# The up projection of a two-layer trunk's MLP as seven block products (Strassen) in place of eight, on one Trainium2 core

## The chip, the cores and the metric

One core of one Trainium2 chip. The time is the device time of one execution of the whole kernel in microseconds (us); the figure is the median of three runs. The engines are named as in the profile: PE multiplies matrices, PEld loads its weights, DVE works on vectors, ACT on activations and copies, POOL on simple vector operations, and SP issues transfers. Each runs its own list of instructions in order, and waits on semaphores of the others.

## The reference, cut to what matters

Two layers; each adds a mixer and a squared-ReLU MLP to a residual `h` of 1024 features and 800 tokens (528 + 272, with 16 meta tokens at the head of each sequence; the second layer's MLP computes the 768 tokens that are put out).

```python
for l in range(DEPTH):
    hn = rms_norm(h, norm_mix[l])
    ...
    h = h + (ym @ w_out[l]).astype(h.dtype)
    hn = rms_norm(h, norm_mlp[l])
    h = h + (jnp.square(jax.nn.relu(hn @ w_up[l])) @ w_down[l]).astype(h.dtype)
return rms_norm(h[:, N_META:], norm_final)
```

`w_up[l]` is 1024 x 4096, `w_down[l]` is 4096 x 1024, all float32.

## The kernel before

Features lie on the 128 partitions and tokens along the free dimension; a tensor of 1024 features is eight tiles `h[0]` to `h[7]` of 128 x 800 (layer 0) or 128 x 768 (layer 1). Tokens are worked on in two halves of 400 or 384 columns. A large product is exact to float32 by three float32r passes: each operand is split into a high part and a low rest (`xh`, `xl` for activations; `wh`, `wl` for weights), and a product is `wh.xh + wh.xl + wl.xh`, the three matmuls of L434, L435 and L436.

Weights come by `raw` (a ring `wr` of three buffers of 512 KB, loaded by a transfer that SP issues, L446), and `wsplit` (L415 to L421) makes `wh` by a copy on ACT (L419) and `wl` by a difference on POOL (L420). Both have rings of two buffers, so a third `wh` waits until PE has done its last matmul with the first. `product` collects its sums in one of three PSUM banks `mm` (a further ring of three is called `hb`) and hands the bank to an eviction.

`mlp` (L1104 to L1181) splits the eight tiles of `h` into `self.x` and goes through w_up's 4096 columns in eight blocks of 512 (four column tiles). `ups(b)` makes four tiles of u: 4 tiles x 2 halves x 8 k x 3 passes = 192 matmuls, an eviction by ACT (relu, L1123) and DVE (times the sum again, L1124), and a split of u by ACT (L1128) and POOL (L1129). `downs(b, us)` takes the 512 rows of w_down in four loads, 8 m x 2 halves x 4 k x 3 = 192 matmuls, and DVE adds each sum to `h[m]` (L1150). `ups(b + 1)` stands ahead of `downs(b)` in the program. The norm's factor is applied late: DVE sums the squares behind `ups(0)` (L1160 to L1164), multiplies `h` by its mean square (L1172), takes the reciprocal (L1173), and multiplies the finished sum by it (L1154).

In layer 0 `s5_setup(1)`, some 400 small operations, most on DVE, is issued behind `downs(0)`; `norm_in` of layer 1 follows as the tiles of `h` are finished, and in layer 1 `final` (L325 to L369) norms and stores them. The order of each engine's list is set at build time by a scheduler with a model of the timeline; buffers of the pools `h`, `m`, `u` and `t` (`FO`) and of the rings come free when their last reader is done.

Of the kernel before, what the change touches and what calls it, by code (L numbers as in the profile page):

```python
# [73 lines left out]
AP = [0, 0]  # L74

class Trunk:
# [82 lines left out]
        # scores of a chunk pair, block-diagonal: the blocks beside the diagonal stay zero  # L159
# [4 lines left out]
        # what leaves the chip for a while  # L164
# [19 lines left out]
        # s5 skip gains: (g2 h) rows, (l gp) columns  # L184
# [6 lines left out]
        # s5 step sizes over the states  # L191
# [9 lines left out]
        # lower bounds: softmax over the depth, running sum less the first  # L201
# [13 lines left out]
        # forget gate = hA*t + hB, key/2 = -hK*t + hK, with t = tanh(x/2)  # L215
# [6 lines left out]
        # rg-lru: softplus(-lambda) with log1p by its atanh series  # L222
# [23 lines left out]
    def gate_weights(self, l):  # L246
        """Block-diagonal gates: (i, d, r|i)."""
# [27 lines left out]
    def load(self):  # L275
        """The residual and the operands of the first w_in, half by half of the tokens."""
# [48 lines left out]
    def final(self, m, t):  # L325
        """The last norm, feature tile by feature tile as they are done."""
        nc = self.nc
        if m == 0:
            self.g = self.t("u", (128, D))
            nc.sync.dma_start(self.g[:], self.ins["norm_final"].rearrange("(a f) -> a f", a=1).to_broadcast([128, D]))  # L330
            self.done, self.early, self.sq = [], [], None
# [16 lines left out]
        if m == 3:  # L348
            for i in range(6):
                o = self.t("t", (128, 512))  # L350
                nc.vector.tensor_tensor(out=o[:], in0=turn(i, 0)[:], in1=self.g[:, 0:512], op=MULT)
                self.early.append(o)
        if m == KD - 1:
# [4 lines left out]
            st = self.t("t", (128, 6))  # L358
# [3 lines left out]
            for i in range(6):  # L362
# [9 lines left out]
    def split(self, k, y, gain, rs=None, n=T):  # L372
        """Operand k = y*gain (*rs) as two float32r parts that add up to it exactly."""
# [12 lines left out]
    def sumsq(self, ys, n=T):  # L386
        """The sum of squares over the partitions of all tiles, on every partition: two PSUM halves."""
# [38 lines left out]
    def product(self, w, xs, halves, evac):  # L426
        """evac(half, psum) with psum = sum over k of w[k].T @ x[k]; w: pairs of [128, 128] parts."""
# [13 lines left out]
    def fetch(self, name, l, c):  # L441
        """128 columns of a weight matrix of 1024 rows, split."""
# [8 lines left out]
    def project(self, l, cols, evacs):  # L451
        """Columns of w_in, 128 from each of cols."""
# [7 lines left out]
    def scaled(self, out):  # L460
        """Evacuation into out, times the tokens' 1/rms."""
# [5 lines left out]
    def gelu(self, x):  # L467
        """x becomes 2 gelu(x), by the tanh formula."""
# [89 lines left out]
    def to_tokens(self, src, dst, dstm):  # L558
        """[feature, token] to [token of a chunk pair, pair, feature]; the meta chunks apart."""
# [37 lines left out]
    def hgrn(self, l, FP, K2, Q, V):  # L597
        """FP: forget gates of both directions, K2: keys, Q, V; returns the heads' outputs, normed."""
# [636 lines left out]
```

## Time and profile before

| | |
|---|---|
| median of three runs | 2200.97 us (2198.35 to 2202.42) |
| span of the profiled execution | 2201.6 us |
| PE busy | 2087.4 us, 95% |
| DVE / ACT / POOL busy | 1118.9 / 753.8 / 811.9 us |
| mean granted clock of PE | 0.964 of full speed |
| matmuls in the trace, all parts | 14082 |
| w_up's three passes in layer 0's windows | 341 to 355 ns recorded each, overlapping |

Busy times are shares of the whole span, over stages with different limits. A record of a matmul is longer than the distance between two of them, because they are pipelined; the pace is the number of matmuls in a window. [...] In a timeline a row stands for one instruction or for several alike ("x3"); "idle before" is how long the engine had nothing to do, and which engine's instruction ended that.

### The profile page before, as it was taken

What the parts mean: (1) busy time and instruction counts of PE and PEld (TensorE: products, weight loads), DVE (VectorE), ACT (ScalarE), POOL (GpSimd) and SP (SyncE); (2) the same over time, 40 slices, a digit from 0 to 9 for tenths busy, and PEclk for the clock granted to TensorE, in tenths of its full rate; (3) what the DMA queues carried; (4) which work ended last, traced back from release to release, by engine and by line L of the source; (5) the groups of instructions that cost most, each with busy time, mean ns of one, the idle gap of its engine ahead of it and who ended that gap; (6) DMA issues with size and microseconds to landing.
All of it is one profiled execution on the core that took longest, in us unless ns stands there. A gap on an engine that the chain in (4) does not pass through costs nothing.

```text
span 2201.6 us, 34495 instructions
## 1 busy us (share of the span) xinstructions
PE 2087.4 (95%) x14082; PEld 1957.7 (89%) x14082; DVE 1118.9 (51%) x2258; ACT 753.8 (34%) x1141; POOL 811.9 (37%) x622
## 2 busy tenths in 40 slices
PE   8899899889989899999999999998998999999998
PEld 6889897677979899999998879886888999999997
DVE  6884748487657871221155855746368221112224
ACT  6233535454322232212225553436432122222222
POOL 1672112263433443333444213322434343434343
PEclk9899899899999999999999999998999999999998
DMA  5322111342211431122122113221321112122221
GB/s 182 96 81 76 38 40 56 101 129 57 68 48 58 109 119 58 58 64 61 58 95 78 57 37 97 74 59 48 113 79 58 58 58 68 59 67 65 60 67 68
DMA packets 230886, 160.74 MB, mean 73 GB/s; under 512 B 33270, under 2 KB 217784, under 8 KB 230728
## 3 DMA queue, kind: packets, MB, share of 16 engines
q1 hardware_dynamic: 229832, 156.95, 23.8%
q8 instruction: 111, 1.82, 0.4%
q10 hardware_dynamic: 896, 1.58, 0.2%
q14 instruction: 47, 0.39, 0.1%
HBM read 131.32 MB, written 27.18 MB: 72 GB/s over the span
## 4 chain that ended last, share of the span: by engine, by line
PE 60%; DVE 10%; ACT 2%; issue 1%; POOL 1%; DMA 1%; SPq 0%; DVEq 0%; POOLq 0%; ACTq 0%
PE mm L435 18%; PE mm L434 18%; PE mm L436 18%; PE hb L664 2%; PE hb L582 1%; DVE m L1163 1%; DVE h L1172 1%; PE rb L510 1%; DVE xl L379 1%; DVE m L1164 1%; DVE h L1154 1%; DVE r L1173 0%; DVE m L1124 0%; PE rb L862 0%; POOL wl L420 0%
## 5 line engine op out<-in xcount | busy, mean ns | idle before, releaser
L420 POOL TENSOR_TENSOR wl<-wr,wh 128x1024 fp32r<-128x1024 f32 (+3 forms) x214 | 479.3, 2240 | 1005.5 <-ACT wh L419 982.7
L434 PE MATMUL mm<-xh,wh 128*128 128x400 f32 (+3 forms) x2016 | 710.2, 354 | 33.1 <-DVE m L1124 11.1
L435 PE MATMUL mm<-xl,wh 128*128 128x400 f32 (+3 forms) x2016 | 713.9, 355 | 6.0 <-POOL xl L383 2.9
L436 PE MATMUL mm<-xh,wl 128*128 128x400 f32 (+3 forms) x2016 | 701.1, 349 | 0.7 <-POOL wl L420 0.5
L419 ACT ACTIVATE wh<-wr 128x1024 fp32r<-128x1024 f32 (+3 forms) x214 | 205.7, 962 | 764.9 <-PE mm L435 658.5
L434 PEld LDWEIGHTS mm<-xh,wh 128*128 128x128 f32 x2016 | 388.6, 193 | 52.7 <-DVE m L1124 14.1
L435 PEld LDWEIGHTS mm<-xl,wh 128*128 128x128 f32 x2016 | 389.1, 193 | 18.5 <-DVE xl L379 4.1
L436 PEld LDWEIGHTS mm<-xh,wl 128*128 128x128 f32 x2016 | 388.8, 193 | 8.9 <-POOL wl L420 0.9
L434 PE MATMUL mm<-u,wh 128*128 128x400 f32 (+1 forms) x1024 | 349.1, 341 | 6.2 <-DVE m L1124 6.2
L435 PE MATMUL mm<-u,wh 128*128 128x400 f32 (+1 forms) x1024 | 349.6, 341 | 0.0
L436 PE MATMUL mm<-u,wl 128*128 128x400 f32 (+1 forms) x1024 | 348.3, 340 | 0.0
L1150 DVE TENSOR_TENSOR h<-mm,h 128x400 f32<-128x400 f32 (+1 forms) x256 | 144.5, 565 | 331.2 <-PE mm L436 331.2
L1124 DVE TENSOR_TENSOR m<-m,mm 128x400 f32<-128x400 f32 (+1 forms) x128 | 71.1, 559 | 369.2 <-ACT m L1123 369.2
L434 PEld LDWEIGHTS mm<-u,wh 128*128 128x128 f32 x1024 | 193.3, 189 | 7.8 <-DVE m L1124 7.1
L435 PEld LDWEIGHTS mm<-u,wh 128*128 128x128 f32 x1024 | 193.2, 189 | 0.1
L436 PEld LDWEIGHTS mm<-u,wl 128*128 128x128 f32 x1024 | 193.1, 189 | 0.1
L1129 POOL TENSOR_TENSOR u<-m,u 128x800 fp32r<-128x800 f32 (+1 forms) x64 | 127.3, 1990 | 53.5 <-ACT u L1128 45.4
L1123 ACT ACTIVATE m<-mm 128x400 f32<-128x400 f32 (+1 forms) x128 | 62.3, 489 | 129.9 <-PE mm L436 115.8
L582 PE MATMUL hb<-hs,hs 64*64 64x64 f32 x2016 | 85.7, 236 | 8.8 <-ACT hs L615 5.6
L582 PEld LDWEIGHTS hb<-hs,hs 64*64 64x64 f32 x2016 | 72.2, 146 | 24.5 <-issue 11.4
L1128 ACT ACTIVATE u<-m 128x800 fp32r<-128x800 f32 (+1 forms) x64 | 55.1, 861 | 83.1 <-DVE m L1124 73.2
L616 DVE TENSOR_TENSOR hd<-hd,hd 128x800 f32<-128x800 f32 (+2 forms) x48 | 43.1, 902 | 13.3 <-ACT hs L614 12.8
(365 smaller groups left out, 2245.8 us busy)
## 6 DMA issues: line engine op xcount, KB each, us to landing
wr<-in_w_up_dram SPq DMA_DIRECT2D x64, 512.0 KB
wr<-in_w_down_dram SPq DMA_DIRECT2D x64, 512.0 KB
wr<-in_w_in_dram SPq DMA_DIRECT2D x46, 512.0 KB
h<-h SPq DMA_DIRECT2D x16, 400.0 KB
wr<-in_w_out_dram SPq DMA_DIRECT2D x32, 192.0 KB
TB<-t SPq DMA_DIRECT2D x24, 200.0 KB
F<-t SPq DMA_DIRECT2D x16, 256.0 KB
E<-t SPq DMA_DIRECT2D x16, 256.0 KB
```

Of the source, the lines that this page charges most:

```text
L419: self.nc.scalar.activation(hi[:], raw, AF.Copy)
L420: self.nc.gpsimd.tensor_tensor(out=lo[:], in0=raw, in1=hi[:].bitcast(F32), op=SUB)
L434: nc.tensor.matmul(ps[:, 0:n], wh, xh[:, c0 : c0 + n], start=(k == 0), stop=False)
L435: nc.tensor.matmul(ps[:, 0:n], wh, xl[:, c0 : c0 + n], start=False, stop=False)
L436: nc.tensor.matmul(ps[:, 0:n], wl, xh[:, c0 : c0 + n], start=False, stop=(k == last))
L582: nc.tensor.matmul(ps[c % 2 * 64 : c % 2 * 64 + 64, c // 2 * 64 : c // 2 * 64 + 64], K[hr, c0 : c0 + 64], Q[hr, c0 : c0 + 64], start=True, ...
L664: mm = lambda out, w, x: nc.tensor.matmul(out, w, x, start=False, stop=False, skip_group_check=True)
L1123: nc.scalar.activation(t[:, sl], ps, AF.Relu)
L1124: nc.vector.tensor_tensor(out=t[:, sl], in0=t[:, sl], in1=ps, op=MULT)
L1128: nc.scalar.activation(u[:, 0], t[:], AF.Copy)
L1129: nc.gpsimd.tensor_tensor(out=u[:, 1], in0=t[:], in1=u[:, 0].bitcast(F32), op=SUB)
L1150: mark = nc.vector.tensor_tensor(out=t[:, sl], in0=ps, in1=t[:, sl], op=ADD)
```

## The change

The MLP goes through w_up in sixteen blocks of 256 columns (two column tiles A and C) in place of eight blocks of 512. In layer 0 blocks 5 to 15, and in layer 1 blocks 2 to 15, are made by `ups7`: the two column tiles, the two halves of k and the two halves of the tokens make a 2 x 2 by 2 x 2 block product, which takes seven products of 4 k x 3 passes = 12 matmuls (Strassen's scheme in Winograd's form), 84 in place of 96. The other blocks keep the plain form with 96.

For it the four combinations of token blocks T1 to T4 are made once for each layer by `sums()` from the parts of `self.x`, on DVE, ACT and POOL; T3 takes the place of the second token half of the first four tiles. For each block DVE makes sums of weight halves (L1185 to L1187, L1190), three and a half splits of weights are made in place of two, and the products are put together from PSUM by DVE (L1205 to L1216, one copy on ACT), squared in SBUF (L1219) and split as before (`as_u`, L1130 and L1131). `downs` loads two pieces of 128x2x512 for a block, and its products are 2 k x 3 passes = 6 matmuls to an eviction (L1238), 512 evictions in all where there were 256. The ring of u holds four tiles; the new pools are `wc` (two), `ws` (one) and `xc` (twelve, from block 4 of layer 0 on, when the `t` pool of `s5_setup` is closed). `norm_in` is called inside `mlp`, and `final` takes its buffers from `xc`. The whole has 9643 PE instructions of matmul where it had 9943. Line numbers of `product` and `wsplit` shift: L419 and L420 are L431 and L432, L434 to L436 are L446 to L448, L1124 is L1142.

```diff
-FO = [['h', 'm', 'u', 't'], ['h', 'm', 'u', 't']]
+FO = [['h', 'm', 'u', 'wc', 'ws'], ['h', 'm', 'u', 'wc', 'ws']]
...
+NS = [5, 2]
...
-        NB = 8
+        NB = 16
...
+        def sums():
...
+            for k in range(4):
+                (ah, al), (ch, cl) = self.x[k], self.x[k + 4]
+                y, z = self.s((128, n)), self.s((128, n))
+                tt(out=y[:], in0=ah[:].bitcast(F32), in1=al[:].bitcast(F32), op=ADD)
+                tt(out=z[:], in0=ch[:].bitcast(F32), in1=cl[:].bitcast(F32), op=ADD)
...
+                tt(out=f[0], in0=y[:, h1], in1=y[:, h0], op=SUB)
+                tt(out=f[1], in0=z[:, h1], in1=f[0], op=SUB)
+                tt(out=f[2], in0=f[1], in1=z[:, h0], op=SUB)
+                tt(out=f[3], in0=z[:, h1], in1=y[:, h1], op=SUB)
+                for o, hi, r in zip(v, his, f):
+                    nc.scalar.activation(hi, r, AF.Copy)
+                    nc.gpsimd.tensor_tensor(out=o, in0=r, in1=hi.bitcast(F32), op=SUB)
...
+        def ups7(b):
...
+            A, C = self.raw((128, KD, 128)), self.t("wc", (128, KD, 128))
...
+            a = self.wsplit(A[:])
+            S = self.t("ws", (128, KD, 128))
+            k0, k1 = slice(0, 4), slice(4, 8)
+            tt(out=S[:, k0], in0=C[:, k0], in1=C[:, k1], op=ADD)
+            tt(out=S[:, k1], in0=S[:, k0], in1=A[:, k0], op=SUB)
+            tt(out=C[:, k0], in0=A[:, k0], in1=C[:, k0], op=SUB)
+            s_ = self.wsplit(S[:])
+            c = self.wsplit(C[:])
+            tt(out=A[:, k1], in0=A[:, k1], in1=S[:, k1], op=SUB)
+            d = self.wsplit(A[:, k1])
...
+            p = mm(self.ps("mm"), a, 0, "11")
+            nc.scalar.activation(t[:, h0], p, AF.Copy)
+            p = mm(self.ps("mm"), a, 4, "21")
+            tt(out=za[:, h0], in0=p, in1=t[:, h0], op=ADD)
+            p = mm(self.ps("mm"), s_, 4, "T2")
+            tt(out=t[:, h1], in0=p, in1=t[:, h0], op=ADD)
+            five = self.ps("hb")
+            p5 = mm(five, s_, 0, "T1")
+            p = mm(self.ps("mm"), c, 0, "T3")
+            tt(out=t[:, h0], in0=p, in1=t[:, h1], op=ADD)
+            tt(out=zc[:, h1], in0=p5, in1=t[:, h0], op=ADD)
+            p = mm(self.ps("hb"), c, 4, "T4")
+            tt(out=zc[:, h0], in0=t[:, h0], in1=p, op=SUB)
+            mm(five, d, 0, "22", start=False)
+            tt(out=za[:, h1], in0=p5, in1=t[:, h1], op=ADD)
+            us = []
+            for z in (za, zc):
+                nc.vector.scalar_tensor_tensor(out=z[:], in0=z[:], scalar=0.0, in1=z[:], op0=ALU.max, op1=MULT)
+                us.append(as_u(z))
+            return us
...
-                for mp in range(2):
-                    raw = self.raw((128, 4, 256))
...
+                raw = self.raw((128, 2, 512))
...
-                        self.product([(hi[:, k, ms_], lo[:, k, ms_]) for k in range(4)], us, halves, ev)
...
+                    self.product([(hi[:, k, ms_], lo[:, k, ms_]) for k in range(2)], us, halves, ev)
...
+                if b + 1 == NS[l]:
...
+                    sums()
+                nxt = (ups if b + 1 < NS[l] else ups7)(b + 1) if b + 1 < NB else None
```

In the order of before, DVE in the middle of layer 0's MLP: the last evictions of one `downs` (`h` from `mm`), those of the next `ups` (`m`), the first of the next `downs`.

```order
L1150 TENSOR_TENSOR h_5099<-mm_8556,h_5099 128x400
L1150 TENSOR_TENSOR h_5099<-mm_8570,h_5099 128x400
L1124 TENSOR_TENSOR m_8590<-m_8590,mm_8591 128x400
L1124 TENSOR_TENSOR m_8590<-m_8590,mm_8618 128x400
L1124 TENSOR_TENSOR m_8654<-m_8654,mm_8655 128x400
```

In the order of after, DVE at the same kind of place, a block of seven products in layer 0; `mm` and `hb` are PSUM, `m` the unfinished u, `wr`, `wc` and `ws` the raw weights A, C and S of the following block.

```order
L1212 TENSOR_TENSOR m_8724<-hb_8768,m_8725 128x400
L1214 TENSOR_TENSOR m_8724<-m_8725,hb_8796 128x400
L1186 TENSOR_TENSOR ws_8979<-ws_8979,wr_8971 128x512
L1187 TENSOR_TENSOR wc_8972<-wr_8971,wc_8972 128x512
L1219 SCALAR_TENSOR_TENSOR m_8724<-m_8724 128x800
L1216 TENSOR_TENSOR m_8723<-hb_8768,m_8725 128x400
L1219 SCALAR_TENSOR_TENSOR m_8723<-m_8723 128x800
L1238 TENSOR_TENSOR h_4885<-mm_8837,h_4885 128x400
L1238 TENSOR_TENSOR h_4885<-mm_8845,h_4885 128x400
```

Every DVE row of before reads PSUM; in after four rows that read SBUF alone stand ahead of the first L1238.

In the order of before, POOL in the same stage: differences of weights and of u in turn.

```order
L420 TENSOR_TENSOR wl_9723<-wr_9720,wh_9722 128x1024
L1129 TENSOR_TENSOR u_9653<-m_9598,u_9653 128x800
L420 TENSOR_TENSOR wl_9787<-wr_9784,wh_9786 128x1024
L1129 TENSOR_TENSOR u_9717<-m_9662,u_9717 128x800
L420 TENSOR_TENSOR wl_9851<-wr_9848,wh_9850 128x1024
```

In the order of after, POOL in one block of seven products: a, s, c, d (half as wide), the two pieces of w_down, and the two tiles of u.

```order
L432 TENSOR_TENSOR wl_8976<-wr_8971,wh_8975 128x1024
L432 TENSOR_TENSOR wl_8984<-ws_8979,wh_8983 128x1024
L432 TENSOR_TENSOR wl_8988<-wc_8972,wh_8987 128x1024
L432 TENSOR_TENSOR wl_8993<-wr_8971,wh_8992 128x512
L432 TENSOR_TENSOR wl_9107<-wr_9104,wh_9106 128x1024
L432 TENSOR_TENSOR wl_9177<-wr_9174,wh_9176 128x1024
L1131 TENSOR_TENSOR u_9097<-m_8996,u_9097 128x800
L1131 TENSOR_TENSOR u_9101<-m_8997,u_9101 128x800
```

The two rows of w_down stand next to each other, and u behind them, where before a row of u followed each row of weights.

In the order of after, POOL in the first block of seven products of layer 0: behind the rows of s and c come the low parts of the token sums, twelve into `xc` and three into `xl`, of which the first four stand here.

```order
L432 TENSOR_TENSOR wl_7619<-ws_7614,wh_7618 128x1024
L432 TENSOR_TENSOR wl_7623<-wc_7607,wh_7622 128x1024
L1170 TENSOR_TENSOR xc_7526<-m_7529,xc_7526 128x400
L1170 TENSOR_TENSOR xc_7527<-m_7529,xc_7527 128x400
L1170 TENSOR_TENSOR xc_7528<-m_7530,xc_7528 128x400
L1170 TENSOR_TENSOR xc_7547<-m_7550,xc_7547 128x400
```

All fifteen are new and stand between the `wl` of c and that of d.

## Rows read from the trace of the kernel before

**Rows 1.** The page: busy time, share and instructions of each engine; the chain by engine.

```profile
PE 2087.4 (95%) x14082; PEld 1957.7 (89%) x14082; DVE 1118.9 (51%) x2258; ACT 753.8 (34%) x1141; POOL 811.9 (37%) x622
...
PE 60%; DVE 10%; ACT 2%; issue 1%; POOL 1%; DMA 1%; SPq 0%; DVEq 0%; POOLq 0%; ACTq 0%
```

**Rows 2.** Windows: from:to, us, busy (count) of each engine, clock, DMA share, GB/s.

```profile
680.00:740.00 60.00, 51.28 (x253) 49.97 (x252) 58.94 (x299) 12.21 (x19) 25.61 (x19) 0.89 0.31 83
740.00:800.00 60.00, 60.00 (x352) 56.78 (x351) 50.64 (x112) 16.94 (x34) 22.19 (x10) 1.00 0.39 116
860.00:920.00 60.00, 60.00 (x331) 60.00 (x330) 12.11 (x22) 12.73 (x16) 22.39 (x10) 1.00 0.19 55
1770.00:1830.00 60.00, 60.00 (x346) 60.00 (x345) 12.24 (x22) 13.26 (x17) 22.22 (x10) 1.00 0.20 62
```

**Rows 3.** PE's waits in 553:640, 640:740 and 1650:1720: us, times, longest.

```profile
PE mm L434 <- DVE m L1124: 4.6, 1, 4.6
PE rb L404 <- DVE m L1164: 4.4, 1, 4.4
PE mm L434 <- DVE m L1098: 2.3, 1, 2.3
...
PE mm L434 <- DVE m L1124: 8.7, 3, 3.7
...
PE rb L404 <- DVE m L1164: 4.6, 1, 4.6
PE mm L434 <- DVE m L1124: 4.0, 1, 4.0
```

**Rows 4.** Groups of 860:920 by form: count, busy us, mean ns, idle before.

```profile
L420 POOL TENSOR_TENSOR wl<-wr,wh 128x1024 fp32r<-128x1024 f32 x7 | 16.8, 2394 | 37.0 <-ACT wh L419 37.0
...
L1150 DVE TENSOR_TENSOR h<-mm,h 128x400 f32<-128x400 f32 x16 | 9.2, 575 | 24.5 <-PE mm L436 24.5
...
L419 ACT ACTIVATE wh<-wr 128x1024 fp32r<-128x1024 f32 x7 | 7.4, 1060 | 40.1 <-PE mm L435 40.1
L1129 POOL TENSOR_TENSOR u<-m,u 128x800 fp32r<-128x800 f32 x3 | 5.7, 1915 | 0.0
```

**Rows 5.** Timeline of DVE at the first MLP's start: start us, us, instruction.

```profile
597.73 0.98 DVE L1163 TENSOR_TENSOR m<-h 128x800 f32<-128x800 f32 x1
...
601.03 6.72 DVE L1163 TENSOR_TENSOR m<-h 128x800 f32<-128x800 f32 x3
...
626.18 5.14 DVE L1173 RECIPROCAL r<-m 128x800 f32<-128x800 f32 x1
```

**Rows 6.** Timeline of POOL, same stretch.

```profile
600.17 2.72 POOL L1129 TENSOR_TENSOR u<-m,u 128x800 fp32r<-128x800 f32 x1 [3.22 <-ACT u L1128]
602.98 3.02 POOL L420 TENSOR_TENSOR wl<-wr,wh 128x1024 fp32r<-128x1024 f32 x1
```

**Rows 7.** Timeline of DVE at the layer border.

```profile
1138.88 2.11 DVE L1154 TENSOR_TENSOR h<-h,r 128x800 f32<-128x800 f32 x1
...
1146.73 2.08 DVE L379 SCALAR_TENSOR_TENSOR xl<-h,pc,xh 128x800 fp32r<-128x800 f32 x1 [0.55 <-ACT xh L378]
...
1149.34 2.10 DVE L1154 TENSOR_TENSOR h<-h,r 128x800 f32<-128x800 f32 x1
```

**Rows 8.** Timeline of POOL at the layer border.

```profile
1144.81 3.16 POOL L420 TENSOR_TENSOR wl<-wr,wh 128x1024 fp32r<-128x1024 f32 x1
1147.92 2.66 POOL L394 TENSOR_TENSOR m<-m,m 128x800 f32<-128x800 f32 x1
```

**Rows 9.** Two 512 KB loads in 880:900: their issue; GB/s in 40 slices of 0.5 us.

```profile
883.35 9.13 SPq L446 DMA_DIRECT2D wr<-in_w_up_dram  x2
...
GB/s 0 0 0 0 0 33 0 0 27 86 188 341 338 69 0 0 0 0 0 0 0 0 0 0 0 0 69 94 276 347 248 14 0 0 0 0 0 0 0 0
```

**Rows 10.** Windows behind two of PE's waits (columns as in the other windows).

```profile
556.00:560.00 4.00, 3.51 (x11) 3.50 (x12) 4.00 (x6) 1.81 (x2) 2.12 (x1) 0.57 0.48 135
...
632.00:638.00 6.00, 6.00 (x26) 5.97 (x27) 0.70 (x2) 1.57 (x3) 3.77 (x2) 0.75 0.22 77
```

More of the change, by code (lines that the diff above doesn't have):

```diff
@@ L95, in phase, with more @@
             self.tags, self.tmp, self.bank = tags, tmp, bank
+            yield
+    @contextmanager
+    def more(self, name, **tags):
+        with ExitStack() as st:
+            for t in tags:
+                self.gp[t] = st.enter_context(self.tc.tile_pool(name=f"{name}_{t}", bufs=1, reuse_waits="tile"))
+            self.tags = {**self.tags, **tags}
             yield
@@ L349, in final @@
             for i in range(6):
-                o = self.t("t", (128, 512))
-                nc.vector.tensor_tensor(out=o[:], in0=turn(i, 0)[:], in1=self.g[:, 0:512], op=MULT)
+                o = self.t("xc", (128, 512))
+                nc.vector.tensor_tensor(out=o[:], in0=turn(i, 0)[:], in1=self.g[0][:], op=MULT)
                 self.early.append(o)
@@ L366, in final @@
                 put(i, 0, o)
-                o = self.t("t", (128, 512))
-                nc.vector.scalar_tensor_tensor(out=o[:], in0=turn(i, 1)[:], scalar=r, in1=self.g[:, 512:1024], op0=MULT, op1=MULT)
+                o = self.t("xc", (128, 512))
+                nc.vector.scalar_tensor_tensor(out=o[:], in0=turn(i, 1)[:], scalar=r, in1=self.g[1][:], op0=MULT, op1=MULT)
                 put(i, 1, o)
@@ L1110, in mlp, with as_u @@
         down = self.ins["w_down"][l]
[L1111 removed]
+        NB = 16
+        w = n // 2
+        h0, h1 = slice(0, w), slice(w, n)
+        X = {}
+        def as_u(t):
+            u = self.t("u", (128, 2, n), F32R)
+            nc.scalar.activation(u[:, 0], t[:], AF.Copy)
+            nc.gpsimd.tensor_tensor(out=u[:, 1], in0=t[:], in1=u[:, 0].bitcast(F32), op=SUB)
+            return u[:, 0], u[:, 1]
         def ups(b):
             us = []
[L1115 to L1130 removed]
@@ new lines, in ups, with ev @@
+            for mi in range(2):
+                t = self.s((128, n))
+                def ev(bb, ps, t=t):
+                    sl = slice(halves[bb][2], halves[bb][2] + halves[bb][1])
+                    nc.scalar.activation(t[:, sl], ps, AF.Relu)
+                    nc.vector.tensor_tensor(out=t[:, sl], in0=t[:, sl], in1=ps, op=MULT)
+                self.product(self.fetch("w_up", l, b * 256 + mi * 128), self.x, halves, ev)
+                us.append(as_u(t))
+            return us
+        def sums():
+            tt = nc.vector.tensor_tensor
+            for q in "11", "21", "22", "T1", "T2", "T3", "T4":
+                X[q] = []
+            for k in range(4):
[3 more added lines that the diff above has]
+                tt(out=z[:], in0=ch[:].bitcast(F32), in1=cl[:].bitcast(F32), op=ADD)
+                T1, T2, T4 = (self.t("xc", (128, 2, w), F32R) for _ in range(3))
+                v = [T1[:, 1], T2[:, 1], T4[:, 1], al[:, h1]]
+                his = [T1[:, 0], T2[:, 0], T4[:, 0], ah[:, h1]]
+                r, q = self.s((128, n)), self.s((128, n))
+                f = [r[:, h0], r[:, h1], q[:, h0], q[:, h1]]
+                tt(out=f[0], in0=y[:, h1], in1=y[:, h0], op=SUB)
[5 more added lines that the diff above has]
+                    nc.gpsimd.tensor_tensor(out=o, in0=r, in1=hi.bitcast(F32), op=SUB)
+                for q, hi, lo in (("11", ah[:, h0], al[:, h0]), ("21", ch[:, h0], cl[:, h0]), ("22", ch[:, h1], cl[:, h1]),
+                                  ("T1", his[0], v[0]), ("T2", his[1], v[1]), ("T4", his[2], v[2]), ("T3", his[3], v[3])):
+                    X[q].append((hi, lo))
@@ L1173, in mlp @@
         nc.vector.reciprocal(r2[:], ms[:])
-        for b in range(NB):
-            nxt = ups(b + 1) if b + 1 < NB else None
-            downs(b, us)
-            if b == 0 and l + 1 < L:
-                with self.using("t", "rb"), self.tc.issue_after(mark.ins):
-                    self.s5_setup(l + 1)
-            us = nxt
+        two = dict(xc=(n, 12))
+        with ExitStack() as st:
+            st.enter_context(self.more("fs", t=(576, 11)) if l + 1 < L else self.more(f"fx{l}", **two))
+            for b in range(NB):
+                if b + 1 == NS[l]:
+                    if l + 1 < L:
+                        st.close()
+                        st.enter_context(self.more(f"fx{l}", **two))
+                    sums()
+                nxt = (ups if b + 1 < NS[l] else ups7)(b + 1) if b + 1 < NB else None
+                downs(b, us)
+                if b == 0 and l + 1 < L:
+                    with self.using("t", "rb"), self.tc.issue_after(mark.ins):
+                        self.s5_setup(l + 1)
+                us = nxt
+            if l + 1 < L:
+                self.norm_in(l + 1, h)
         return h
@@ L1196, in run @@
                 self.mix(l)
-            with self.phase(f"f{l}", {k: dict(h=(T, 8), m=(T, 4), u=(2 * T, 8), t=(576, 11))[k] for k in FO[l]}, "m", "rb"):
-                h = self.mlp(l, self.mix_out(l))
-                if l + 1 < L:
-                    self.norm_in(l + 1, h)
+            with self.phase(f"f{l}", {k: dict(h=(T, 8), m=(T, 4), u=(2 * T, 4), wc=(D, 2), ws=(D, 1))[k] for k in FO[l]}, "m", "rb"):
+                self.mlp(l, self.mix_out(l))
 def trunk_kernel(tc, ins, outs):
```

60 lines of the change are left out of this document (29 added, 31 removed).

## The prediction

> **What bounds the kernel now.** I read the page's busy times first, then the windows by stage, then the waits of PE, and last the single rows of DVE and POOL. PE is busy for 95% of the span and has 60% of the chain that ended last [rows 1], so removed matmuls are worth their full pace wherever PE never waits. That pace is read from whole windows, not from the length of a record, since matmuls overlap. In the middle of the first layer's MLP 331 matmuls fill 60 us with the clock at 1.00, 0.1813 us for each product of 400 columns; in the second layer 346 fill 60 us, 0.1734 us for 384 columns [rows 2]. In both windows PE is busy for all of the 60 us, and DVE for 12 of them. So the body of the MLP is bound by PE, and any wait put in front of PE there is new time. PE's few waits are at the start of each MLP and in the stretch where `s5_setup` fills DVE [rows 3].
>
> **What the change removes.** Eleven blocks of layer 0 and fourteen of layer 1 take 84 matmuls for two tiles in place of 96. 11 x 12 x 0.1813 + 14 x 12 x 0.1734 = 23.9 + 29.1 = 53.0 us, if PE never waits for more than it does now.
>
> [...] The measured pace stands in my sum.
>
> **What it adds in every block.** Four sums of weight halves on DVE (L1185, L1186, L1187, L1190, 128x512 each, both inputs in SBUF), six combinations from PSUM, two relu-squares of 128x800 with SBUF inputs alone, 1.5 more splits of weights on ACT and POOL, and twice as many evictions of half the length of gathering (L1238). By busy time all this fits: on POOL 5 x 2.39 + 1.3 + 2 x 1.92 = 17.1 us and on DVE about 17 us [rows 4], beside 180 x 0.1813 = 32.6 us of PE. The transfers are as large as before. What doesn't fit is the order on DVE.
>
> The trace of before shows that a DVE operation whose inputs all lie in SBUF and a POOL product don't overlap. Alone, an 800-wide one takes 0.98 us; three in a row beside two POOL products took 6.72, while those two took 2.72 and 3.02 [rows 5, 6] and not the 1.92 and 2.39 of [rows 4]. The pattern is exact: the 800-wide `xl` that starts at 1146.73 ends at 1148.81, 0.84 us behind the end at 1147.97 of POOL's product [rows 7, 8], and the next 800-wide row takes 2.10 again, while evictions from PSUM keep their 0.575 [rows 4]. So a DVE operation of this kind waits for POOL's running product and then takes its own streaming time, 0.85 us for 800 columns and, scaled, 0.55 for 512; then POOL gets its next product in before DVE's next.
>
> [...]
>
> In the new order DVE has L1214, then L1186 and L1187 (the next block's weight sums), L1219, L1216, L1219, and only then the first eviction of the running `downs`; this is so in 9 blocks of layer 0 and 12 of layer 1. Beside them POOL has the two 1024-wide `wl` of this block's w_down. I follow one block by hand, with time 0 where the last product (22) can start, T4's end being 0.16:
>
> - ACT's `wh` of the first w_down piece takes T3's buffer: 0.25 to 1.31 (1.06 [rows 4]); POOL's `wl` 1.39 to 3.78. The second `wh` waits for the end of product 22 (12 x 0.1813 = 2.18) and ends near 3.5, so POOL's second `wl` is ready before the first is done.
> - DVE's L1214 0.25 to 0.82. L1186 wants the next block's A, whose transfer is issued when POOL has read the old one for d. T1 ends at -4.18, then `wh` and `wl` of d, half as wide as those of [rows 4] and estimated at 0.62 and 1.3, end at -2.07; the transfer takes 4.1 us (issued at 883.35, moving until about 887.5 [rows 9]): there at 2.1. By then POOL is in its product, so L1186 ends at 3.78 + 0.55 = 4.33.
> - POOL's second `wl` 4.33 to 6.72, and L1187 waits for it: 7.27. Now POOL is idle: L1219 to 8.25, L1216 to 8.8, L1219 to 9.8, the first eviction to 10.37.
> - PE's first three groups of `downs` fill the ring of three `mm` banks; the fourth needs the first one's eviction. Undisturbed it would start at 2.18 + 18 x 0.1813 = 5.44; now at 10.45. PE stands still for 5.0 us (5.1 in layer 1, with shorter matmuls).
>
> After a wait of PE the rows show half clock: the 4 us behind the 2.3 us wait have 11 matmuls in 3.51 us at clock 0.57 where 19 belong, and the 6 us behind the 4.6 us wait that ended before 632 have 26 at 0.75 where 33 belong [rows 3, 10]: 7 or 8 matmuls, another 1.3 to 1.5 us. I take 1.5, and 1.7 for the upper end. A block loses 6.5 us (6.6): 9 x 6.5 + 12 x 6.6 = **+138 us**. The last block of each layer has no L1186 and L1187, its first eviction ends near 6.5, about 1 us late: +2 for both.
>
> **What it adds at the edges.** Each from nearby rows, with both ends:
> - First seven-product block of layer 0. T1 to T4 wait for 15 POOL differences of 128x400 (about 1.07, from 1.92 at 800 and 2.39 at 1024) that stand behind the `wl` of c, which waits for product 21. 1.15 + 2.4 + 15 x 1.07 = 19.6, and the DVE sums that alternate with them bring it to 20 to 28 us, against 48 matmuls (8.7) of PE work; a delayed first eviction follows. +27, ends 10 and 36.
> - The same sums in layer 1, partly beside earlier blocks: +20, ends 5 and 30.
> - Start of each MLP. DVE's chain of norm and rescaling, 597.7 to 631.3 (its first and last row in [rows 5]), now has 192 matmuls (35 us) ahead of the first eviction in place of 384. PE waited 4.6 + 4.4 us in layer 0, 4.6 + 4.0 in layer 1 [rows 3]. +10 and +12, ends 0 and 20 each.
> - `s5_setup`: DVE is busy for 58.9 of 60 us there and PE waits 8.7 [rows 2, 3]. Two blocks' worth of evictions more, about 32 x 0.57 = 18 us, go into it. +16; 0 if the next window's free tenth (50.6 of 60 busy) takes it up, 25 with half clock.
> - Layer border: `norm_in` takes 10.46 us for two tiles (1138.88 to 1149.34 [rows 7]), 5.2 each, as DVE and POOL alternate; the last block's PE work beside it falls from 4.35 to 2.17 us a tile. 8 x 2.17 = 17 at most. +13, ends 5 and 17.
> - `final` in the same manner with half the cover, on DVE alone: +4, ends 0 and 8.
>
> **Sum.** -53 + 138 + 2 + 27 + 20 + 22 + 16 + 13 + 4 = +189. The profiled execution's span is 2201.6 us, the median 2201.0, so nothing is to be shifted: **2390 us**. With all low ends of the edges and 1.3 for the clock 2304, with all high ends 2450.
>
> **The rivals.**
> - *DVE slips L1186 and L1187 between the two POOL products.* For it: between them POOL waits for its `wh`, and if that comes a little later both sums pass in one gap. Then L1187 ends at 4.9, the first eviction at 8.0; the stall is 2.6 us and half clock about 0.8: 21 x 3.4 = 71 in place of 138, so 2323. Against it: POOL took its turn after one DVE row each time in [rows 5 to 8], and the second `wh` is done before the first `wl`.
> - *No exclusion in these rows* (sums of 128x4x128 blocks might not count as the 800-wide rows do). Then A's landing at 2.1 sets the chain, the eviction ends at 6.3, and the stall is 0.9 us without a change of clock: 21 x 0.9 = 19. The edges, half of them made by alternation, come to about 52: 2201 - 53 + 19 + 2 + 52 = 2221; if they shrink to a third, 2200, no change.
> - *Faster: the chain is covered.* If A is there before L1214 is done (0.82) and POOL doesn't get in between, the six operations and the eviction take 0.55 + 0.55 + 0.98 + 0.55 + 0.98 + 0.57 = 4.2 and end at 5.0, before the 5.44 at which PE needs the bank. It decides at 0.4 us. With edges of 10 to 30 the time is 2160 to 2180. For it: DVE is half empty. Against it: A's transfer can start only when its old reader on POOL is done, and lands at 2.1.
>
> **How the numbers follow.** The forecast has 0.72, the slip 0.12, no exclusion 0.09 (0.06 at about 2221, 0.03 at no change), the covered chain 0.07. Within 0.2% (4.4 us) counts as the same, about what a measurement of this kernel can tell from no change. Faster 0.07, same 0.03, slower 0.90. The range 2285 to 2450 holds the forecast with its ends and the slip, and leaves out the last two cases.
>
> **What would show it.** In the profile after: PE waits in the 21 blocks, once each, for DVE L1238, 4 to 5 us long, with clock below 1 right behind; L1186 and L1187 of over 2 us, each ending about 0.55 behind a POOL row; L1238 still 0.56. In the windows of a steady block PE busy for about 32 to 35 us of 39. Wrong at once: L1186 at 0.6 us, or no wait of PE for L1238. If steady blocks show 32.6 us and the time is still above 2200, the edges were the price and not the order on DVE. Were PE to wait for POOL's `wl` or for a transfer, the resource would be another than mine.

## The result and the profile after

The changed kernel takes 2420.2 us (2413.5 to 2422.8), the kernel before 2199.7: a ratio of 1.099, 95% interval 1.097 to 1.101. Slower by 220 us, where +189 was forecast; it lies within the range.

The page of the changed kernel, its busy times and its chain by engine, to be held against [rows 1]:

```profile
PE 2143.7 (89%) x13782; PEld 1980.2 (82%) x13782; DVE 1540.8 (64%) x2762; ACT 780.4 (32%) x1148; POOL 954.7 (39%) x704
...
PE 46%; DVE 22%; DMA 5%; issue 2%; ACT 2%; POOL 1%; DVEq 0%; SPq 0%; POOLq 0%; ACTq 0%
```

PE has 300 matmuls fewer and is busy for 56 us *more*: its mean granted clock is 0.917, where it was 0.964. DVE, 10% of the chain before, is 22% of it now.

PE's waits in the steady blocks of layer 0 (860 to 1230 us) and of layer 1 (1880 to 2400 us), engine and line waited for, us, times, longest:

```profile
PE mm L446 <- DVE h L1238: 34.0, 9, 3.8
PE mm L448 <- POOL wl L432: 2.8, 10, 0.7
...
PE mm L446 <- DVE h L1238: 45.4, 12, 3.8
PE mm L448 <- POOL wl L432: 4.9, 13, 0.7
```

Nine waits and twelve, one a block, all for the first eviction of `downs`: the 21 places that the order had shown. The second line of each pair, 0.3 to 0.4 us a block, is a wait for POOL's first `wl` of w_down, which the chain by hand had left out. In these stretches of the kernel before there were no waits.

DVE's timeline in one block of layer 0, start us, us, instruction, and what ended idle time before it:

```profile
1015.90 0.57 DVE L1214 TENSOR_TENSOR m<-m,hb 128x400 f32<-128x400 f32 x1 [0.64 <-PE hb L1198]
1017.37 2.49 DVE L1186 TENSOR_TENSOR ws<-ws,wr 128x512 f32<-128x512 f32 x1 [0.89 <-DMA wr<-in_w_up_dram]
1019.78 2.87 DVE L1187 TENSOR_TENSOR wc<-wr,wc 128x512 f32<-128x512 f32 x1
1022.57 0.98 DVE L1219 SCALAR_TENSOR_TENSOR m<-m 128x800 f32<-128x800 f32 x1
1023.47 0.56 DVE L1216 TENSOR_TENSOR m<-hb,m 128x400 f32<-128x400 f32 x1
1024.07 0.99 DVE L1219 SCALAR_TENSOR_TENSOR m<-m 128x800 f32<-128x800 f32 x1
1024.98 1.53 DVE L1238 TENSOR_TENSOR h<-mm,h 128x400 f32<-128x400 f32 x3
```

POOL's timeline at the same place; "x2" is the pair of `wl` of w_down:

```profile
1016.91 5.19 POOL L432 TENSOR_TENSOR wl<-wr,wh 128x1024 fp32r<-128x1024 f32 x2 [3.50 <-ACT wh L431]
```

PE at the same place, the last matmul ahead of the wait and the first behind it:

```profile
1021.49 0.34 PE L448 MATMUL mm<-u,wl 128*128 128x400 f32 x1
1025.60 0.70 PE L446 MATMUL mm<-u,wh 128*128 128x400 f32 x1 [3.77 <-DVE h L1238]
```

L1186 and L1187 are records of 2.49 and 2.87 us for sums of 512 columns. POOL's pair ends at 1022.10, and L1187 at 1022.65, 0.55 us behind it, the streaming time that the prediction had scaled from 800 columns. L1186 waited 0.89 us for A's transfer first, and then for POOL: it ends at 1019.86, and POOL's first `wl`, 2.40 us from 1016.91 on, at 1019.31. The first eviction follows four more operations later. Only the sizes differ a little from the hand chain: with time 0 (where product 22 can start) at 1015.65, the first eviction ends at 9.9 and not at 10.4.

Windows of the changed kernel, from:to, us, busy time (count) of PE, PEld, DVE, ACT and POOL, granted clock, DMA share, GB/s: eight steady blocks of layer 0, eleven of layer 1, and stretches around one wait (PE's last matmul ahead of it ends at 1021.83, the first behind it starts at 1025.60):

```profile
860.60:1174.60 314.00, 281.88 (x1442) 276.26 (x1441) 164.18 (x225) 64.64 (x72) 139.70 (x65) 0.93 0.17 52
1906.70:2319.80 413.10, 367.68 (x1981) 360.63 (x1980) 218.31 (x308) 88.13 (x99) 190.05 (x89) 0.95 0.18 55
...
1021.00:1024.00 3.00, 0.82 (x5) 0.49 (x3) 3.00 (x3) 0.00 (x0) 1.10 (x1) 1.00 0.56 202
1024.00:1030.00 6.00, 4.40 (x13) 4.36 (x14) 3.04 (x6) 1.63 (x2) 3.75 (x2) 0.53 0.15 58
1030.00:1040.00 10.00, 10.00 (x53) 9.99 (x53) 5.68 (x10) 1.06 (x1) 2.41 (x1) 0.94 0.00 0
...
1025.60:1031.00 5.40, 5.40 (x16) 5.35 (x17) 2.05 (x4) 1.12 (x2) 3.75 (x2) 0.50 0.00 0
1032.00:1040.00 8.00, 8.00 (x46) 8.00 (x45) 4.80 (x9) 1.06 (x1) 2.41 (x1) 1.00 0.00 0
```

A block takes 314.0 / 8 = 39.25 us in layer 0 and 413.1 / 11 = 37.55 in layer 1, where the matmuls alone need 32.63 and 31.21: 6.6 and 6.3 us lost, 6.5 and 6.6 forecast. It is made up differently, though: PE stands still for 4.0 us (314.0 - 281.88 over eight), not 5.0, and is busy for 35.2 us over work of 32.6, so half clock behind the wait costs 2.6 us and not 1.5; in layer 1 the two are 4.1 and 2.2 us. Behind the wait shown, PE's granted clock is 0.50 of full speed for the 5.4 us from 1025.60 to 1031, and it does 16 matmuls where 30 belong; from 1032 on the clock is 1.00 again.

The whole difference of the two profiled spans, 218.1 us, by stages. A stage's loss is its length less its matmuls at the pace of [rows 2], and the table has the loss after less that before:

| stage | forecast | measured |
|---|---|---|
| 300 matmuls fewer | -53.0 | -53.0 |
| 21 steady blocks | +138 | +135.7 |
| last blocks without L1186, L1187 | +2 | +2.1 |
| layer 0: MLP start, `s5_setup`, first seven-product block | +53 | +50.5 |
| layer 1: MLP start and token sums | +32 | +29.5 |
| layer border: last block of layer 0, up to the mixer's first small products | +13 | +12.8 |
| the rest of layer 1's mixer | 0 | +32.2 |
| end of layer 1, `final` | +4 | +7.0 |
| ahead of the first MLP | 0 | +4.3 |
| unforecast: 0.4 us that each block of before had over its matmuls | 0 | -3 |

The stretch ahead of the first MLP is from 562 to 578 us long in the eight kernels below and the two above, though it is the same code, so its 4.3 us are no finding. Each figure is from one execution of each kernel. The 32.2 us of the mixer stand out; the runs on layer 1 below tell how far.

### The profile page after: what moved, and what is told of

Read it like the earlier page. It is cut to its first block, busy times and chain, and to the rows that moved or that the text cites. A ratio compares the mean times of both kernels' runs of the same rounds, so it can differ in the third digit from the quotient of the medians.

```text
span 2419.7 us, 34522 instructions
## 1 busy us (share of the span) xinstructions
PE 2143.7 (89%) x13782; PEld 1980.2 (82%) x13782; DVE 1540.8 (64%) x2762; ACT 780.4 (32%) x1148; POOL 954.7 (39%) x704
## 4 chain that ended last, share of the span: by engine, by line
PE 46%; DVE 22%; DMA 5%; issue 2%; ACT 2%; POOL 1%; DVEq 0%; SPq 0%; POOLq 0%; ACTq 0%
PE mm L446 10%; PE mm L447 9%; PE mm L448 9%; DMA wr<-in_w_up_dram 4%; DVE wc L1187 3%; PE mm L1197 3%; PE mm L1196 3%; PE mm L1198 3%; DVE ws L1186 2%; DVE h L1238 2%; DVE m L1219 2%; PE hb L676 2%; PE hb L594 1%; DVE h L1242 1%; PE hb L1197 1%
## 5 line engine op out<-in xcount | busy, mean ns | idle before, releaser
L432 POOL TENSOR_TENSOR wl<-wr,wh 128x1024 fp32r<-128x1024 f32 (+3 forms) x214 | 461.1, 2161 | 715.3 <-ACT wh L431 688.3
L446 PE MATMUL mm<-u,wh 128*128 128x400 f32 (+1 forms) x1024 | 377.6, 369 | 139.5 <-DVE h L1238 127.5
L446 PE MATMUL mm<-xh,wh 128*128 128x400 f32 (+3 forms) x1216 | 443.6, 368 | 25.7 <-DVE m L1110 7.8
L447 PE MATMUL mm<-xl,wh 128*128 128x400 f32 (+3 forms) x1216 | 439.6, 362 | 3.7 <-POOL xl L395 1.8
L448 PE MATMUL mm<-xh,wl 128*128 128x400 f32 (+3 forms) x1216 | 434.7, 359 | 0.7 <-POOL wl L432 0.5
L1238 DVE TENSOR_TENSOR h<-mm,h 128x400 f32<-128x400 f32 (+1 forms) x512 | 281.9, 561 | 200.1 <-PE mm L448 199.9
L431 ACT ACTIVATE wh<-wr 128x1024 fp32r<-128x1024 f32 (+3 forms) x214 | 195.2, 913 | 624.1 <-issue 211.5
L448 PE MATMUL mm<-u,wl 128*128 128x400 f32 (+1 forms) x1024 | 361.2, 361 | 7.7 <-POOL wl L432 7.7
L446 PEld LDWEIGHTS mm<-u,wh 128*128 128x128 f32 x1024 | 208.5, 204 | 156.8 <-DVE h L1238 142.0
L446 PEld LDWEIGHTS mm<-xh,wh 128*128 128x128 f32 x1216 | 240.6, 198 | 45.0 <-issue 9.3
L447 PEld LDWEIGHTS mm<-xl,wh 128*128 128x128 f32 x1216 | 241.2, 198 | 15.5 <-POOL xl L395 3.1
L448 PEld LDWEIGHTS mm<-xh,wl 128*128 128x128 f32 x1216 | 240.1, 198 | 8.3 <-POOL wl L432 0.9
L448 PEld LDWEIGHTS mm<-u,wl 128*128 128x128 f32 x1024 | 207.6, 203 | 15.4 <-POOL wl L432 15.1
L1131 POOL TENSOR_TENSOR u<-m,u 128x800 fp32r<-128x800 f32 (+1 forms) x64 | 122.2, 1926 | 161.4 <-ACT u L1130 156.3
L432 POOL TENSOR_TENSOR wl<-ws,wh 128x1024 fp32r<-128x1024 f32 x25 | 62.8, 2510 | 151.3 <-ACT wh L431 151.3
L1130 ACT ACTIVATE u<-m 128x800 fp32r<-128x800 f32 (+1 forms) x64 | 52.2, 852 | 213.8 <-DVE m L1219 141.0
L1197 PE MATMUL mm<-xl,wh 128*128 128x384 f32 (+1 forms) x300 | 103.7, 346 | 0.0
L1196 PE MATMUL mm<-xh,wh 128*128 128x384 f32 (+1 forms) x300 | 103.2, 344 | 0.3 <-ACT m L1203 0.3
```

The source lines that it names most:

```text
L431: self.nc.scalar.activation(hi[:], raw, AF.Copy)
L432: self.nc.gpsimd.tensor_tensor(out=lo[:], in0=raw, in1=hi[:].bitcast(F32), op=SUB)
L446: nc.tensor.matmul(ps[:, 0:n], wh, xh[:, c0 : c0 + n], start=(k == 0), stop=False)
L447: nc.tensor.matmul(ps[:, 0:n], wh, xl[:, c0 : c0 + n], start=False, stop=False)
L448: nc.tensor.matmul(ps[:, 0:n], wl, xh[:, c0 : c0 + n], start=False, stop=(k == last))
L1131: nc.gpsimd.tensor_tensor(out=u[:, 1], in0=t[:], in1=u[:, 0].bitcast(F32), op=SUB)
```

## The experiments

The theory is the one on record: DVE's SBUF-only operations ahead of the first eviction and POOL's products of w_down exclude one another. The rivals were that DVE's queue is too long whatever POOL does, and that A's transfer is late, for which L1186 waits. Four runs separate them.

**The low parts of w_down left out.** From block 5 of layer 0 and 2 of layer 1 on, POOL makes no `wl` for w_down, and PE takes `wh` a second time.

```diff
-                hi, lo = self.wsplit(raw[:])
+                hi, lo = self.wsplit(raw[:], b < NS[l])
...
-                    self.product([(hi[:, k, ms_], lo[:, k, ms_]) for k in range(2)], us, halves, ev)
+                    self.product([(hi[:, k, ms_], (lo or hi)[:, k, ms_]) for k in range(2)], us, halves, ev)
```

> Leaves out the low parts of w_down in the blocks whose next block is a seven-product one: POOL makes no wl for these pieces, and PE multiplies by wh a second time, so its work and DVE's order stay. Exclusion theory (DVE's L1186 and L1187 wait for these two POOL products): both sums fall from 2.2 to 2.9 us to about 0.7, the first eviction ends near 5.5 us after product 22 can start in place of 9.9, PE's wait for it is under 1 us, a steady block of layer 0 takes 33 to 34 us in place of 39.3, and the time is about 2285. Rival 'DVE's queue is simply too long': nothing changes on DVE, blocks stay at 38 to 39, time about 2410. Rival 'the transfer of A is late': sums are short but start where they did or later, blocks 35 to 38.

Measured 2274.3 us (ratio to before 1.033, 1.028 to 1.037). Steady blocks take 32.7 us in layer 0, hardly more than the 32.63 of their matmuls, and 31.6 in layer 1. DVE's timeline there:

```profile
1013.38 0.69 DVE L1189 TENSOR_TENSOR ws<-ws,wr 128x512 f32<-128x512 f32 x1 [1.08 <-DMA wr<-in_w_up_dram]
1013.99 0.69 DVE L1190 TENSOR_TENSOR wc<-wr,wc 128x512 f32<-128x512 f32 x1
1014.59 0.98 DVE L1222 SCALAR_TENSOR_TENSOR m<-m 128x800 f32<-128x800 f32 x1
1015.49 0.57 DVE L1219 TENSOR_TENSOR m<-hb,m 128x400 f32<-128x400 f32 x1
1015.98 0.56 DVE L1241 TENSOR_TENSOR h<-mm,h 128x400 f32<-128x400 f32 x1
```

The two sums (L1189 and L1190 in this kernel) take 0.69 us each, although A's transfer still comes as late (1.08 us of waiting). The first eviction ends at 1016.5, 4.8 us behind the start of L1217 (L1214 of the changed kernel, where it was 9.6). From the start of the first sum to the end of the second it takes 1.3 us where it took 5.3, so 4.0 of the 4.8 us that the chain got shorter are theirs. So neither the transfer nor the number of operations made the stall, but POOL's two products beside the sums: the exclusion is shown for these rows. DVE's order is the same but for one relu-square, which stands behind the first eviction here; that takes 1 us off the chain and isn't the exclusion's.

**The sums behind the sixth eviction**, POOL untouched:

```diff
-            tt(out=S[:, k1], in0=S[:, k0], in1=A[:, k0], op=SUB)
-            tt(out=C[:, k0], in0=A[:, k0], in1=C[:, k0], op=SUB)
+            with self.tc.issue_after(evs[5].ins):
+                tt(out=S[:, k1], in0=S[:, k0], in1=A[:, k0], op=SUB)
+                tt(out=C[:, k0], in0=A[:, k0], in1=C[:, k0], op=SUB)
...
+                        evs.append(mark)
```

> The two weight sums L1186 and L1187 of the next block are issued behind the sixth eviction of the running down product; all else stays. Exclusion theory: now the first relu-square waits for POOL (to about 4.6) and the second too (7.9), the first eviction ends near 8.4; PE's wait falls from 3.8 to about 2.5 us, blocks from 39.3 to about 36.5, time about 2360. Rival 'the transfer of A is late' (the sums are the only rows that wait for it): the wait is gone, blocks 33, time about 2285. Rival 'queue too long': two of seven operations less, 1.4 us gained, time about 2385.

Measured 2291.0 us (1.040, 1.032 to 1.048), blocks of 33.6 and 32.4 us: far better than the theory's 36.5, and close to what the rival of the late transfer had said. The first run has excluded that rival; the timelines tell where my chain went wrong. DVE and POOL at that place:

```profile
1015.36 0.57 DVE L1215 TENSOR_TENSOR m<-m,hb 128x400 f32<-128x400 f32 x1 [0.64 <-PE hb L1199]
1015.97 0.99 DVE L1220 SCALAR_TENSOR_TENSOR m<-m 128x800 f32<-128x800 f32 x1
1017.54 0.57 DVE L1217 TENSOR_TENSOR m<-hb,m 128x400 f32<-128x400 f32 x1 [0.57 <-PE hb L1199]
1018.15 1.92 DVE L1220 SCALAR_TENSOR_TENSOR m<-m 128x800 f32<-128x800 f32 x1
1020.31 2.02 DVE L1240 TENSOR_TENSOR h<-mm,h 128x400 f32<-128x400 f32 x3 [0.24 <-PE mm L448]
```

```profile
1016.37 5.96 POOL L432 TENSOR_TENSOR wl<-wr,wh 128x1024 fp32r<-128x1024 f32 x2 [3.50 <-ACT wh L431]
```

The first relu-square (L1220) starts at 1015.97, 0.4 us *before* POOL's first product, and takes 0.99; only the second, which starts while POOL's pair is running, has to wait (1.92). I had let POOL go first. The exclusion is the same, but in this block the relu-square that started first kept its time. POOL's pair takes 5.96 us here and 5.19 in the changed kernel, where [rows 4] have 2.39 for one product. In the changed kernel L1214 ends at 1016.47, POOL's first product starts at 1016.91, and L1186 only at 1017.37, when A has come. So the late transfer may have a part in the stall after all, by letting POOL start first; that is inferred, since no run has A there earlier. What a block loses here, 1 us, is for the most part PE's wait for POOL's `wl` (860 to 1160 us):

```profile
PE mm L448 <- POOL wl L432: 6.2, 9, 0.7
```

**The squares on ACT**, the sums where they were:

```diff
-                nc.vector.scalar_tensor_tensor(out=z[:], in0=z[:], scalar=0.0, in1=z[:], op0=ALU.max, op1=MULT)
+                nc.scalar.activation(z[:], z[:], AF.Relu)
+                nc.scalar.activation(z[:], z[:], AF.Square)
```

> The relu-squares go from DVE to ACT (relu, then square, two passes of each u tile); the weight sums stay where they are. Exclusion theory: L1186 and L1187 still wait for POOL's two products (end near 7.3), then only L1216 stands ahead of the first eviction, which ends near 8.4; blocks about 36.5, time about 2360. Rival 'queue too long': 2 us gained, blocks 37, the same time, but with L1186 and L1187 read at 2 us or more it is the exclusion. Rival 'transfer of A late': blocks 37 to 38.

Measured 2341.8 us (1.063, 1.056 to 1.070), blocks of 36.3 on average in layer 0 (36.9 and 35.3) and 34.1 in layer 1. L1186 and L1187 still read 2.2 and 2.9 us in the median, and PE's wait for the first eviction is 1.9 us a block (its rows in 860 to 1180 us):

```profile
PE mm L446 <- DVE h L1239: 16.8, 9, 1.9
PE mm L448 <- POOL wl L432: 2.2, 9, 0.2
```

The wait is half as long as in the changed kernel (3.8), and of the 6.6 us a block 3.7 remain. This is as the chain by hand had it: the two relu-squares, 2 us, are off DVE, and the sums still take 2.2 and 2.9 us.

**Both edits:**

> Both: the sums behind the sixth eviction and the squares on ACT, so no DVE operation on SBUF alone stands ahead of the first eviction. Exclusion theory: the first eviction ends at about 3.3 us, PE doesn't wait, blocks 32.7 to 33.5 in layer 0 and 31.3 to 32 in layer 1, time about 2280; what is left over the kernel before, about 80, is then the price of the edges less 53. Rival: if PE or its clock has another limit in these blocks, they stay above 35.

Measured 2277.0 us (1.034, 1.029 to 1.039); blocks of 33.2 and 32.0 us. One block's length of layer 0, columns as above:

```profile
1017.40:1050.60 33.20, 32.94 (x182) 32.61 (x182) 15.02 (x26) 11.27 (x15) 17.14 (x8) 1.00 0.20 64
```

PE busy all but 0.26 us, at a clock of 1.00, with POOL's work unchanged at 17 us. The price of the order on DVE in the 21 blocks is thus 21 x some 5.8 = 122 us of the 220. What is left, some 74 us over the kernel before, is the edges and the mixer less the gain. The other three runs and one more take those apart.

**Sixteen plain blocks, no seven products** (`NS = [16, 16]` in place of `[5, 2]`):

> Sixteen blocks of 256 columns, all with the plain eight products; pools as in the changed kernel, no sums. It measures the halved blocks by themselves. Edge prices of the prediction: +22 for the two starts, +16 for s5_setup, +13 border, +4 end: about 2256, plus some 30 if the mixer is reordered here too: 2285. A steady block takes 34.9 us (layer 0) and 33.4 (layer 1) if doubled evictions cost nothing in the body. Rival: halved blocks cost in the body as well (eviction of 0.57 for every 1.09 us of PE): over 36.

Measured 2286.1 us (1.038, 1.032 to 1.043). Steady blocks 34.9 and 33.5 us: 192 x 0.1813 = 34.8, so doubled evictions are free in the body, as forecast. Halved blocks cost at the edges alone.

How much they cost there can't be read straight from this run: unlike what was expected of it, it isn't without sums. The program calls `sums()` where `b + 1 == NS[l]`, which with 16 holds in the last block of each layer: the token sums are made beside it, for no product. POOL's rows of them in layer 0 (1125 to 1200 us), and PE's waits there and in the blocks ahead (760 to 1125 us):

```profile
L1170 POOL TENSOR_TENSOR xc<-m,xc 128x400 fp32r<-128x400 f32 x12 | 16.5, 1388 | 13.4 <-ACT xc L1169 13.4
...
PE mm L446 <- DVE h L1238: 13.6, 7, 4.6
...
PE mm L446 <- DVE h L1238: 0.6, 2, 0.3
```

From the end of block 13 on, layer 0's MLP takes 75.6 us here and 61.2 in the run with both edits, and layer 1 to the end of the kernel 89.3 and 75.9. Less the 12 matmuls more of a plain last block, the sums cost an estimated 12 and 11 us. Layer 0's MLP is 630.5 us long (594.7 before), from its first eviction of an up product to its last of a down product, layer 1's 561.4 (542.3), the tail behind that 25.5 (18.1), and the mixer between them 499.0 (477.3). Without the sums, halved blocks would cost some 39 us at the edges, where the forecast had 55, and the kernel would take about 2262 us. So 2286 agrees with the 2285 expected by luck.

It also follows, as an estimate, that the seven products don't pay even with both edits: that run took 2277.0 us, and leaving its mixer aside it is some 8 us longer than halved blocks alone. The 53 us of matmuls saved go into the token sums and the first block that needs them, some 50 us in both layers, and into 0.5 to 0.8 us that each seven-product block still takes over its matmuls.

**Layer 1 alone**, layer 0's MLP as before; and the same **with both edits** of above:

> Layer 0's MLP exactly as in the kernel before (eight blocks of 512), layer 1's as in the changed kernel. It tells where the mixer of layer 1, 38.6 us longer in the changed kernel from the last eviction of layer 0 to the first of layer 1's MLP, gets its time. If layer 0's new MLP (its border, its pools) causes it: 477 us again, time 2201 + 80 + 3 = about 2284. If it is the scheduler's order of the mixer, which differs in every build I listed: some other length, 500 to 515, time about 2310. Layer 1's MLP itself 622 us in both cases.

> As the run with layer 1 alone, with the sums behind the sixth eviction and the squares on ACT. Exclusion theory: layer 1's MLP about 552 us as in the run with both edits (542.3 before), the tail 3 longer: 2214 us with a mixer of 477, 2245 with one of 506. Faster than before only if the start of the MLP loses less without layer 0's change, which nothing suggests.

Measured 2284.8 us (1.037, 1.032 to 1.043) and 2217.7 (1.0069, 1.0036 to 1.0102). Layer 1's MLP takes 623.6 and 551.7 us, against 621.8 in the changed kernel and 542.3 before: the parts add up. The mixer of layer 1 is back, at 483.4 and 477.2 us, as the first of the two cases had it: layer 0's new MLP causes its extra time. The expectation had PE's order as different in every kernel; over the mixer alone it is the same in these two, item for item, as in the kernel before. In the changed kernel and the run with both edits it is another one (the same in these two), in the runs with the sums moved and without seven products yet others. Rows of the whole mixer, from the last eviction of layer 0 to the first of layer 1's MLP, columns as above; first the kernel before:

```profile
1163.90:1641.20 477.30, 455.81 (x3831) 397.59 (x3832) 285.94 (x473) 220.88 (x341) 144.29 (x151) 0.96 0.24 70
```

the changed kernel:

```profile
1261.20:1777.10 515.90, 484.07 (x3850) 423.39 (x3849) 299.41 (x477) 224.54 (x343) 144.24 (x152) 0.90 0.23 68
```

both edits:

```profile
1197.30:1703.70 506.40, 476.85 (x3850) 417.90 (x3849) 299.66 (x477) 224.70 (x343) 143.94 (x152) 0.92 0.23 69
```

layer 1 alone with both edits:

```profile
1161.40:1638.60 477.20, 456.16 (x3831) 397.06 (x3832) 287.50 (x474) 221.32 (x341) 144.39 (x151) 0.96 0.24 72
```

The work is nearly the same (3831 and 3850 matmuls in the trace, 3 us more), and ACT's and POOL's busy times agree within 4 us; DVE is busy for 13 us longer, six of them for four rows of the border that fall into this window. But PE is busy for 28 us longer in the changed kernel and idle for 10 us longer, at a mean clock of 0.90 against 0.96. 515.9 x 0.10 - 477.3 x 0.04 = 32.5 us of full-clock time. So the unforecast 32 us go with another order of the mixer's products, in which PE's mean clock is lower; nothing of the mixer was edited. The same order doesn't always take the same time: the four kernels with the order of before have mixers of 477.2 to 483.4 us, the two with that of the changed kernel 506.4 and 515.9. So at least 23 us go with the order, and up to ten differ between two kernels that share it. The scheduler orders it behind what the new MLP of layer 0 leaves. That this order by itself, and not the state in which the MLP leaves the buffers, makes the difference is not shown: no run has the old order behind the new MLP.

**Seven products from block 4 of layer 1 on** in place of block 2, else as the last run (`NS = [5, 4]`):

> As the fixed version of layer 1 alone, but seven products from block 4 on in place of block 2, so that the token sums have two more plain blocks to hide beside. If the sums' price (some 19 us in layer 1: start to end of block 1 takes 113 us against 95 without seven products) comes only from their standing close to the first block that needs them: 2 blocks x 1.5 us less gain, some 10 to 15 us of the 19 back, MLP of layer 1 about 541 us, time 2200 to 2206, no difference to the kernel before. If it comes from the DVE and POOL work itself wherever it stands: 2214 to 2220.

Measured 2224.6 us beside 2208.8 for the kernel before (1.0074, 1.0045 to 1.0103). The sums don't hide: the blocks at which they stand take 42.1 and 40.9 us instead of 33.5 and 32.0, so 17.5 us of the 19 are paid again, and two blocks' gain, 3 us, is lost. PE's waits there (1735 to 1820 us) are for an eviction queued behind the sums, and for ACT's high parts of them:

```profile
PE mm L446 <- DVE h L1320: 5.9, 2, 5.3
PE hb L1276 <- ACT xc L1248: 4.8, 1, 4.8
```

No version tried beats the kernel before. The best, layer 1 alone with both edits, is 0.7% slower (0.4 to 1.0%).

## Why the prediction was right, step by step

The pace, and -53.0 with it, is right by construction; the run without seven products confirms the 34.9 us of a plain block.

The **steady blocks** are the forecast's largest term and came within 2 us of it: +135.7 for +138. The mechanism is shown by the first run, but two sizes in it were off and cancelled, so the close number is in part luck. PE stands still for 4.0 us and not 5.0, since the chain ends half a microsecond earlier and the first three groups take 3.8 us where I had 3.3: PE waits in them for POOL's first `wl`, for which the chain by hand had no wait. Half clock costs 2.2 to 2.6 us and not 1.5. The windows from which I took the 1.5 [rows 10] end 4 and 6 us behind the wait. Here the 4.4 us from 1025.6 to 1030 hold 13 matmuls where 24 belong, 2.0 us, and the 10 us behind them lose 0.6 more at 0.94.

One row was misread: the traffic in [rows 9] ends at 887.0 and not at 887.5, so the transfer takes 3.6 us and not 4.1. A is there at 1.7 on the hand chain's clock and not at 2.1. Nothing hangs on it here, since POOL's first product had started at 1.3.

The **rival of the slip** didn't occur: POOL took its turn after the first of the two rows, and L1186 and L1187 both wait (2.49 and 2.87 us). The **rival without exclusion** is excluded by 2.49 and 2.87 us against 0.69. The **covered chain** had two conditions, an early A and no POOL in between. With the second alone (the first run, where A is as late as it was) a block takes 32.7 us, so that one is nearly enough: with the relu-square that stands behind the eviction there, the chain would end an estimated 0.6 us behind the 5.44 at which PE needs the bank. Whether an early A would do by itself, by letting L1186 start ahead of POOL, no run tells.

The **first block of layer 0, the start and `s5_setup`** together are +50.5 for +53; layer 1's start and sums +29.5 for +32. The run without seven products gives the parts, since its sums stand in other blocks: layer 1's start alone is 16.0 us over its matmuls where before lost 8.7, so 7 for the forecast 12, and the sums the other 22 for 20. In layer 0 start and `s5_setup` come to about 18 for 26, and sums and first block to 33 for 27. So here too the totals are closer than their terms: the starts were put too high and the sums too low. The **border** is 12.8 for 13.

The step that failed is one that wasn't taken: the text holds no term for layer 1's **mixer**, since the diff doesn't touch it, and reads the new order only in the MLP. It cost 32 us in the profiled execution, a seventh of the whole, about as much as the 30 us between 2390 and 2420. That the mixer's order is a new one could have been read from PE's list; its price stands in no row of the trace of before. What in the new order or behind the new MLP makes it stays open.

The expectation of the second run let POOL go first, as the chain by hand does. There the first relu-square, 0.4 us ahead of POOL's first product, took 0.99 us, and POOL's pair 5.96 where two products of [rows 4] take 4.78.

## What to carry to other kernels

Here 53 us of saved matmuls were outweighed by 136 us of stalls, because short operations on another engine stood in front of an eviction that PE needs: look, in the new order, at every operation between the last product and the first eviction, and ask which of them can wait for POOL or for a transfer. Work for a later block belongs behind the evictions, and moving two rows of DVE there gave back some 113 us in the 21 blocks here. Count, too, what a scheme needs once per layer: the token sums ate what the seven products saved. And a change that reorders one stage can make a scheduler reorder the next; list that order too, and look at the clock of the stages that were not edited.

## What the runs showed of the hardware

- In the places shown, DVE operations with both inputs in SBUF and POOL's products took turns. DVE's sum of 512 columns took 0.69 us with POOL's products left out. Beside them, in the changed kernel, L1186 and L1187 read 2.49 and 2.87 us and ended 0.55 us behind POOL's first and second `wl`. POOL's records stretch in the same way: two `wl`, 2.39 us each in [rows 4], took 5.19 us there and 5.96 in the run with the sums moved.
- In the run with the sums moved, the relu-square that started 0.4 us ahead of POOL's pair took 0.99 us, as in the changed kernel with POOL idle (L1219, 0.98 and 0.99), and the one that started while the pair ran took 1.92. An eviction from PSUM beside the same pair took 0.57 (L1217).
- After a wait of 3.8 us in the changed kernel PE's granted clock was 0.50 of full speed for the next 5.4 us, and 1.00 in the 8 us from 1032 on. A steady block's PE was busy for 2.2 to 2.6 us more than its matmuls need at full clock, more than half of its wait of 4.0 to 4.1 us again.
- The mixer's mean clock was 0.96 with one order of its products and 0.90 and 0.92 with another, at nearly the same work (3831 and 3850 matmuls in the trace). That the order alone makes the difference is not shown.
